# An encoder block on one core: the gated product gets a tile of its own, and the handling of w_down is tied to the rounds of the up projection

## Chip, cores, metric

One of the cores of a Trainium2 chip runs the whole program. The metric is the device time of one execution in microseconds (us). Engines are named as in the profile: PE (TensorE), DVE (VectorE), ACT (ScalarE), POOL (GpSimd), and SP, whose instruction queue issues every DMA of this kernel.

## What is computed

The block has three sub-layers: a mixer of a convolution group and an attention group, a cross-attention into 256 memory tokens, and a gated MLP. The change touches the last:

```python
def conv_gated_ffn(h, w_up, ffn_dw, ffn_dw_b, w_down):
    u = jnp.einsum("bsd,df->bsf", h, w_up)                 # h: 1024 tokens x 1024
    u = dwconv_centred(u, ffn_dw, ffn_dw_b)                # width 3 along the tokens
    gate, val = u[..., :D_FF], u[..., D_FF:]               # D_FF = 2816
    return jnp.einsum("bsf,fd->bsd", jax.nn.gelu(gate, approximate=True) * val, w_down)
```

All of it is float32. The kernel keeps that precision by splitting each operand into a high and a low part and doing three matmuls per product.

## The kernel before, in words

**Up projection.** The 2816 gate channels and the 2816 value channels are taken 128 at a time, in 22 *rounds* (`NF`). In a round the result for one channel block is a matrix `u` of 128 channels x 2 (gate, value) x 1024 tokens. The multiplication of [gate; value] weights by [first half; second half] of the model dimension and by two halves of the tokens is done with seven products instead of eight (Strassen's scheme in Winograd's form). Each product is 12 matmuls of 128 x 128 by 128 x 512, its result one PSUM bank (`psB`, 4 buffers). The right operands `b11, b21, b22, t1..t4` are made once, before the rounds; the left operands `a1, a2, a3, a22` are made in each round from the two loaded weight tiles `wg` and `wv`.

- `up_first(fi)` (L788): load `wg`, split it into `a1` (high part ACT, low part POOL), products p1 and p2. p1 is copied to `q`, p2 + q is the first half of the gate.
- `up_operands(fi)` (L803): load `wv`; POOL makes the sums `s12`, `s34`; `a_split` (L774) makes `a2` and `a3` (high part ACT, low part DVE) and `a22` (ACT, POOL).
- `up_finish(fi)` (L832): products p6, p5, p3, p7, p4. Their partial sums go through `q`, a tile of 128 x 1024 from the pool `tmpp` (4 buffers, also used by `s12` and `s34`), until both halves of `u` are there; then `conv3` (L822: one ACT and two DVE instructions into PSUM) on each half, gelu on ACT, and the product of the two, written over `u[:, 1]` (L859) and stored to DRAM as `act_d[fi]` (L860).

`u`, `a1`, `a2`, `a3` and `a22` share the pool `wp` of 7 buffers. `wg` and `wv` share `rawp` (3 buffers) with other raw tiles.

**Preparing the down projection.** It uses the same seven-product scheme and needs four differences of blocks of `w_down`. They are made during the up projection, in 22 pieces: `down_load(fi)` (L763) brings a piece of 512 KB into one half of `wd_b`, `down_sums(fi)` (L766) does four subtractions of 128 x 256 on DVE in place (L769), `down_store(fi)` (L771) writes it to `T_d` in DRAM. `wd_b` has two halves, so piece fi+2 is loaded when piece fi has been stored.

**Down projection.** Seven products m1, m2, m6, m7, m5, m4, m3, each a sum over 11 blocks `i` of 12 matmuls (L91 to L93, results `yd`). The left operands come from `acts`, eleven tiles that are loaded from `act_d` in two halves each (L895, L897) into buffers that the right operands of the up projection leave; the right ones (`st`, L913) come from `w_down` or `T_d`, two blocks a load. Each is split by one ACT (L930) and one DVE instruction (L920).

**What sets the order.** A list scheduler places the instructions on the five queues at compile time by a timeline of its own; each engine then runs its queue strictly in order, and waits are semaphores. Nothing in the code before ties `down_load`, `down_sums` and `down_store` to a round, so the scheduler sets them as soon as its timeline finds them possible.

Of the kernel before, what the change touches and what calls it, by code (L numbers as in the profile page):

```python
# [11 lines left out]
ALU = mybir.AluOpType  # L12
# [5 lines left out]
NF = 22  # L18
# [16 lines left out]
def encoder_block(ctx: ExitStack, tc: tile.TileContext, x, xT, mem, w_a, w_q, w_kv, w_mkv, w_mqT,  # L35
                  w_mo, w_out, w_up, w_down, cols, rows, g10, rope, out):
    nc = tc.nc
# [10 lines left out]
    def A(shape, name, dt=F32R):  # L48
        return ap.tile([128] + shape, dt, tag="a", name=name)

    def raw(name):
        return rawp.tile([128, 1024], F32, tag="raw", name=name)

    def tmp(name):
        return tmpp.tile([128, 1024], F32, tag="tmp", name=name)

    def psS(name):
        return psp.tile([128, 1024], F32, tag="S", name=name, bufs=2)

    def psB(name):  # L60
        return psp.tile([128, 512], F32, tag="B", name=name, bufs=4)
# [4 lines left out]
    def f(t):  # L66
        return t.bitcast(F32)
# [10 lines left out]
    def cc(i):  # L78
        return col[:, i:i + 1]
# [31 lines left out]
    def W(shape, name):  # L111
        return wp.tile([128] + shape, F32R, tag="w", name=name)
# [150 lines left out]
    for t in range(2):  # L263
        r = raw(f"mem{t}")
# [135 lines left out]
    for i in range(2):  # L400
        r = raw(f"wkv{i}r").rearrange("p (k n) -> p k n", k=4)
# [3 lines left out]
        for j in (2 * i, 2 * i + 1):  # L405
            r = raw(f"wq{j}r").rearrange("p (k n) -> p k n", k=2)
# [211 lines left out]
    def post_norm(y, gB, resid, name):  # L618
# [5 lines left out]
        nc.vector.tensor_tensor(out=t, in0=t, in1=resid, op=ALU.add)  # L624
        return t

    def load_raw(src, name):
        r = raw(name)
        nc.sync.dma_start(out=r, in_=src)
        return r  # L630

    def transpose_split(src, dh, dl, tt):
# [80 lines left out]
    def cross_gemm(t):  # L713
        y = psS("y2")
        tok_gemm(y, Ph[t // 4], Pl[t // 4], Uw, t % 4)
        return y, load_raw(x1_d[t], "x1r")
# [36 lines left out]
    act_d = drp.tile([NF, 128, 1024], F32, name="act_d")  # L753


    T_d = drp.tile([NF // 2, 128, 4, 512], F32, name="T_d")

    wd_b = A([2, 4, 256], "wd", F32)

    def down_slice(dr, fi):  # L760
        return dr[fi // 2, :, :, fi % 2 * 256:fi % 2 * 256 + 256]

    def down_load(fi):  # L763
        nc.sync.dma_start(out=wd_b[:, fi % 2], in_=down_slice(w_down, fi))

    def down_sums(fi):  # L766
        b11, b12, b22, b21 = [wd_b[:, fi % 2, b, :] for b in range(4)]
        for dst, in0, in1 in ((b11, b12, b11), (b12, b22, b12), (b22, b22, b11), (b21, b22, b21)):
            nc.vector.tensor_tensor(out=dst, in0=in0, in1=in1, op=ALU.subtract)  # L769

    def down_store(fi):  # L771
        nc.sync.dma_start(out=down_slice(T_d, fi), in_=wd_b[:, fi % 2])

    def a_split(dst, src, eng):  # L774
        nc.scalar.copy(out=dst[:, 0, :], in_=src)  # L775
        eng.tensor_tensor(out=dst[:, 1, :], in0=src, in1=f(dst[:, 0, :]), op=ALU.subtract)  # L776

    def product(ps, a, b):
        bh, bl = BO[b]
        for k in range(4):  # L780
            ks = slice(k * 128, k * 128 + 128)
            gemm3_multi([ps], (a[:, 0, ks], a[:, 1, ks]), [(bh[:, k, :], bl[:, k, :])], k == 0, k == 3)

    a22 = [None, None]
    H0, H1 = slice(0, 512), slice(512, 1024)
    ups, firsts, rgs = {}, {}, {}

    def up_first(fi):  # L788

        rg = rgs.pop(fi) if fi in rgs else load_raw(w_up[fi, 0], "wg")  # L790
        a1 = W([2, 2, 512], "a1")
        a_split(a1[:, 0], rg[:, H0], nc.gpsimd)
        a_split(a1[:, 1], rg[:, H1], nc.gpsimd)
        u = wp.tile([128, 2, 1024], F32, tag="w", name="u")
        q = tmp("q")
        p1, p2 = psB("p1"), psB("p2")
        product(p1, a1[:, 0], "b11")
        nc.scalar.copy(out=q[:, H0], in_=p1)
        product(p2, a1[:, 1], "b21")
        nc.vector.tensor_tensor(out=u[:, 0, H0], in0=p2, in1=q[:, H0], op=ALU.add)  # L800
        firsts[fi] = (rg, u, q)

    def up_operands(fi):  # L803

        rg, u, q = firsts.pop(fi)
        rv = load_raw(w_up[fi, 1], "wv")
        s12, s34 = tmp("s12"), tmp("s34")
        nc.gpsimd.tensor_tensor(out=s12[:, H0], in0=rv[:, H0], in1=rv[:, H1], op=ALU.add)
        nc.gpsimd.tensor_tensor(out=s12[:, H1], in0=s12[:, H0], in1=rg[:, H0], op=ALU.subtract)
        nc.gpsimd.tensor_tensor(out=s34[:, H0], in0=rg[:, H0], in1=rv[:, H0], op=ALU.subtract)  # L810
        nc.gpsimd.tensor_tensor(out=s34[:, H1], in0=rg[:, H1], in1=s12[:, H1], op=ALU.subtract)
        a2, a3 = W([2, 2, 512], "a2"), W([2, 2, 512], "a3")
        a_split(a2[:, 0], s12[:, H1], nc.vector)
        a_split(a2[:, 1], s12[:, H0], nc.vector)
        a_split(a3[:, 0], s34[:, H1], nc.vector)
        a_split(a3[:, 1], s34[:, H0], nc.vector)
        if fi % 2 == 0:
            a22[0] = W([2, 2, 512], "a22")
        a_split(a22[0][:, fi % 2], rv[:, H1], nc.gpsimd)
        ups[fi] = (a2, a3, a22[0][:, fi % 2], u, q)  # L820

    def conv3(fi, gv, u):  # L822
        ci = gv * NF + fi
        c = psS("c")
        nc.scalar.activation(out=c, in_=u[:, gv], func=AF.Identity, scale=cc(C_FDW + ci * 3 + 1), bias=cc(C_FDB + ci))  # L825
        nc.vector.scalar_tensor_tensor(out=c[:, 1:], in0=u[:, gv, :S - 1], scalar=cc(C_FDW + ci * 3), in1=c[:, 1:],  # L826
                                       op0=ALU.mult, op1=ALU.add)
        nc.vector.scalar_tensor_tensor(out=c[:, :S - 1], in0=u[:, gv, 1:], scalar=cc(C_FDW + ci * 3 + 2),
                                       in1=c[:, :S - 1], op0=ALU.mult, op1=ALU.add)
        return c  # L830

    def up_finish(fi):  # L832
        a2, a3, a22_, u, q = ups.pop(fi)

        def add(dst, ps, other, op=ALU.add, swap=False):
            nc.vector.tensor_tensor(out=dst, in0=other if swap else ps, in1=ps if swap else other, op=op)  # L836

        p6, p5 = psB("p6"), psB("p5")
        if fi == 0:
            product(p5, a2[:, 1], "t1")  # L840
        product(p6, a2[:, 0], "t2")
        add(q[:, H0], p6, q[:, H0])
        if fi:
            product(p5, a2[:, 1], "t1")
        add(q[:, H1], p5, q[:, H0])
        p3 = psB("p3")
        product(p3, a3[:, 0], "b22")
        add(u[:, 0, H1], p3, q[:, H1])
        p7 = psB("p7")
        product(p7, a3[:, 1], "t3")  # L850
        add(q[:, H0], p7, q[:, H0])
        add(u[:, 1, H1], p5, q[:, H0])
        cg = conv3(fi, 0, u)
        nc.scalar.activation(out=u[:, 0], in_=cg, func=AF.Gelu_apprx_tanh)
        p4 = psB("p4")
        product(p4, a22_, "t4")
        add(u[:, 1, H0], p4, q[:, H0], op=ALU.subtract, swap=True)
        cv = conv3(fi, 1, u)
        nc.vector.tensor_tensor(out=u[:, 1], in0=u[:, 0], in1=cv, op=ALU.mult)  # L859
        nc.sync.dma_start(out=act_d[fi], in_=u[:, 1])  # L860

    UP_PRE = 2
    for t in range(8):
        if t == 6:
            for fi in range(UP_PRE):
                rgs[fi] = load_raw(w_up[fi, 0], "wg")
        j = cross_norm(t, *cross_gemm(t))
        if t == 7:
            for fi in range(UP_PRE):
                up_first(fi)  # L870
        cross_operands(t, j)
    for fi in range(NF + 1):
        if fi < NF:
            if fi >= UP_PRE:
                up_first(fi)
            up_operands(fi)
        if fi == 0:
            down_load(0)
        else:
            down_store(fi - 1)  # L880
            up_finish(fi - 1)
        if fi < NF:
            down_sums(fi)
        if fi + 1 < NF:
            down_load(fi + 1)

# [205 lines left out]
```

## Time and profile before

| | us |
|---|---|
| median of 3 runs (1451.33 to 1456.73) | 1452.29 |
| profiled execution | 1453.6 |
| its span | 1451.5 |
| PE busy | 1383.5 (95%) |
| DVE busy | 1070.8 (74%) |
| ACT busy | 699.9 (48%) |
| POOL busy | 514.0 (35%) |

The span is the time from the first to the last instruction; around it lie 2.1 us. A stretch of the span is read with a table of windows (busy time and number of instructions of each engine, granted clock of PE, share of the DMA engines); an idle place with the timeline of an engine, which gives the idle time before an instruction and what ended it; and the way in which one delay leads to the next with the chain of work, followed back from the end.

### The profile page before, as it was taken

The numbers are of one execution on the slowest core, as the hardware profiler recorded it, in microseconds if no ns is written. First come the engines' busy times: TensorE is split into PE (matmuls) and PEld (weight loads), VectorE is DVE, ScalarE is ACT, GpSimd is POOL, SyncE is SP. The second block draws the span as 40 slices with busy tenths as digits, with TensorE's granted clock in tenths as the row PEclk, the third lists the DMA queues.
The fourth block names the chain that finished last, engine by engine and source line by source line (L and its number), as shares of the span: only waits on it lengthen the run. The fifth ranks groups of instructions, "written<-read, shape, count | busy, mean of one in ns | idle before, by whom it ended". The sixth has DMA issues, their size and how long they took to land.

```text
span 1451.5 us, 18836 instructions
## 1 busy us (share of the span) xinstructions
PE 1383.5 (95%) x7042; PEld 1167.5 (80%) x7042; DVE 1070.8 (74%) x1442; ACT 699.9 (48%) x1191; POOL 514.0 (35%) x506
## 2 busy tenths in 40 slices
PE   9999999799999999999996989789999999999996
PEld 7889988679898888888885767678888888888885
DVE  6699899799998334335458878877777778985576
ACT  7426543588888434334444424234444443544452
POOL 5548887600102324002136525345554441000003
PEclk9999999999999999999998999899999999999998
DMA  6417750000000434013223576742222228622325
GB/s 236 135 59 238 243 200 14 19 1 2 30 1 12 163 103 151 24 43 131 87 87 102 174 232 198 236 135 83 74 93 81 88 87 317 226 88 88 109 87 210
DMA packets 74060, 170.08 MB, mean 117 GB/s; under 512 B 9713, under 2 KB 32497, under 8 KB 73969
## 3 DMA queue, kind: packets, MB, share of 16 engines
q1 hardware_dynamic: 73968, 168.88, 35.1%
q8 instruction: 55, 0.90, 0.3%
q14 instruction: 37, 0.30, 0.1%
HBM read 124.82 MB, written 44.04 MB: 116 GB/s over the span
## 4 chain that ended last, share of the span: by engine, by line
PE 62%; DVE 7%; DMA 5%; ACT 2%; issue 2%; POOL 1%; POOLq 0%; DVEq 0%; ACTq 0%; SPq 0%
PE p L98 7%; PE p L99 6%; PE p L101 6%; PE yd L91 5%; PE yd L92 5%; PE yd L93 5%; PE y L99 4%; PE y L101 4%; PE y L98 4%; PE pPT L82 3%; DVE wd L769 3%; DMA wd<-in_w_down_dram 2%; DMA T_d<-wd 2%; PE sc L101 2%; PE sc L98 2%; PE sc L99 2%
## 5 line engine op out<-in xcount | busy, mean ns | idle before, releaser
L305 DVE SCALAR_TENSOR_TENSOR cacc<-conv,col,cacc 128x1009 f32<-128x1009 f32 (+14 forms) x120 | 145.8, 1276 | 4.7 <-ACT cacc L253 4.5
L86 POOL TENSOR_SCALAR rt<-ss 128x1 f32<-128x1 f32 (+1 forms) x43 | 15.0, 349 | 353.5 <-DVE ss L920 227.2
L92 PE MATMUL yd<-op 128*128 128x512 f32 x308 | 119.8, 389 | 0.0
L93 PE MATMUL yd<-op 128*128 128x512 f32 x308 | 119.7, 389 | 0.0
L775 ACT CAST a<-s 128x512 fp32r<-128x512 f32 x88 | 50.8, 621 | 105.6 <-PE p L101 65.1
L91 PE MATMUL yd<-op 128*128 128x512 f32 x308 | 96.9, 389 | 0.0
L930 ACT CAST op<-acts 128x512 fp32r<-128x512 f32 x77 | 48.0, 624 | 99.6 <-PE yd L93 87.8
L776 POOL TENSOR_TENSOR a<-wg,a 128x512 fp32r<-128x512 f32 x44 | 63.1, 1456 | 84.1 <-ACT a L775 84.0
L920 DVE TENSOR_TENSOR op<-acts,op 128x512 fp32r<-128x512 f32 x77 | 53.1, 690 | 46.5 <-ACT op L930 46.4
L826 DVE SCALAR_TENSOR_TENSOR c<-u,col,c 128x1023 f32<-128x1023 f32 x44 | 56.6, 1285 | 39.9 <-ACT c L825 39.9
L557 DVE TENSOR_TENSOR PL<-pPT,PH 128x512 fp32r<-128x512 f32 x128 | 83.2, 681 | 2.4 <-ACT PH L556 1.4
L539 DVE TENSOR_REDUCE nm<-sp 128x1 f32<-128x1024 f32 x64 | 78.0, 1218 | 7.3 <-PE sp L537 6.8
L825 ACT ACTIVATE c<-u,col 128x1024 f32<-128x1024 f32 x44 | 53.2, 1209 | 54.8 <-DVE u L836 53.4
L542 ACT ACTIVATE P<-sp,nm 128x1024 f32<-128x1024 f32 x64 | 72.2, 1128 | 15.4 <-PE pPT L82 6.5
L776 DVE TENSOR_TENSOR a<-s,a 128x512 fp32r<-128x512 f32 x88 | 67.0, 779 | 15.2 <-ACT a L775 15.0
L556 ACT CAST PH<-pPT 128x512 fp32r<-128x512 f32 x128 | 69.4, 593 | 13.9 <-PE pPT L82 13.4
L769 DVE TENSOR_TENSOR wd<-wd 128x256 f32<-128x256 f32 x88 | 57.0, 664 | 20.5 <-DMA wd<-in_w_down_dram 20.0
L82 PE MATMUL pPT<-ident,P 128*128 128x128 f32 x512 | 67.9, 273 | 0.7 <-DVE PL L557 0.7
L92 PEld LDWEIGHTS yd<-op 128*128 128x128 f32 x308 | 57.8, 188 | 12.4 <-DVE op L920 0.4
L91 PEld LDWEIGHTS yd<-op 128*128 128x128 f32 x308 | 57.8, 188 | 12.0
L93 PEld LDWEIGHTS yd<-op 128*128 128x128 f32 x308 | 57.8, 188 | 12.0
L776 POOL TENSOR_TENSOR a<-wv,a 128x512 fp32r<-128x512 f32 x22 | 32.9, 1513 | 97.5 <-ACT a L775 83.1
(344 smaller groups left out, 4395.1 us busy)
## 6 DMA issues: line engine op xcount, KB each, us to landing
wg<-in_w_up_dram SPq DMA_DIRECT2D x22, 512.0 KB, 4.4
wv<-in_w_up_dram SPq DMA_DIRECT2D x22, 512.0 KB, 4.2
wd<-in_w_down_dram SPq DMA_DIRECT2D x22, 512.0 KB, 4.2
T_d<-wd SPq DMA_DIRECT2D x22, 512.0 KB, 3.9
act_d<-u SPq DMA_DIRECT2D x22, 512.0 KB, 2.9
acts<-act_d SPq DMA_DIRECT2D x22, 512.0 KB, 6.8
st<-T_d SPq DMA_DIRECT2D x20, 512.0 KB, 3.7
wmkv_r<-in_w_mkv_dram SPq DMA_DIRECT2D x16, 512.0 KB, 4.1
```

The source lines that it names most:

```text
L82: nc.tensor.transpose(out=out_, in_=in_, identity=ident)
L91: nc.tensor.matmul(out=ps, lhsT=sh, rhs=mh, start=first, stop=False)
L92: nc.tensor.matmul(out=ps, lhsT=sh, rhs=ml, start=False, stop=False)
L93: nc.tensor.matmul(out=ps, lhsT=sl, rhs=mh, start=False, stop=last)
L98: nc.tensor.matmul(out=p, lhsT=sh, rhs=mh, start=first, stop=False)
L99: nc.tensor.matmul(out=p, lhsT=sh, rhs=ml, start=False, stop=False)
L101: ins = nc.tensor.matmul(out=p, lhsT=sl, rhs=mh, start=False, stop=last)
L305: nc.vector.scalar_tensor_tensor(out=acc[:, t0:t1_], in0=a[:, t0 + o:t1_ + o], scalar=cc(C_DW + c * 31 + j), in1=acc[:, t0:t1_], op0=ALU.m ...
L539: nc.vector.reduce_max(out=nm, in_=sp, axis=AX.X, negate=True)
L557: nc.vector.tensor_tensor(out=PL[dst], in0=p3, in1=f(PH[dst]), op=ALU.subtract)
L769: nc.vector.tensor_tensor(out=dst, in0=in0, in1=in1, op=ALU.subtract)
L776: eng.tensor_tensor(out=dst[:, 1, :], in0=src, in1=f(dst[:, 0, :]), op=ALU.subtract)
```

## The change

1. `q` is no longer a tile of `tmpp` but the value half of `u`, `u[:, 1, :]`. The gated product goes to a new tile `o` of `tmpp`, and `act_d[fi]` is stored from `o`.
2. `down_load` and `down_store` are queued on SP behind the last load of `wg` or `wv` that the program text issued (`issue_after` adds an edge of order on the engine's own queue, no semaphore).
3. `down_sums(fi + 1)` is called within `up_finish(fi)` and queued on DVE behind the addition of p7; piece 0 behind the last split of `up_operands(0)`. `down_store(fi - 2)` stands behind `up_first(fi)`, `down_load(fi)` behind `up_operands(fi)`; the last two stores follow the loop.

```diff
+    last_load = [None]
     def load_raw(src, name):
         r = raw(name)
-        nc.sync.dma_start(out=r, in_=src)
+        last_load[0] = nc.sync.dma_start(out=r, in_=src)
...
     def down_load(fi):
-        nc.sync.dma_start(out=wd_b[:, fi % 2], in_=down_slice(w_down, fi))
-    def down_sums(fi):
+        with tc.issue_after(last_load[0].ins):
+            nc.sync.dma_start(out=wd_b[:, fi % 2], in_=down_slice(w_down, fi))
+    def down_sums(fi, behind):
...
+        with tc.issue_after(behind.ins):
+            for dst, in0, in1 in ((b11, b12, b11), (b12, b22, b12), (b22, b22, b11), (b21, b22, b21)):
+                nc.vector.tensor_tensor(out=dst, in0=in0, in1=in1, op=ALU.subtract)
     def down_store(fi):
-        nc.sync.dma_start(out=down_slice(T_d, fi), in_=wd_b[:, fi % 2])
+        with tc.issue_after(last_load[0].ins):
+            nc.sync.dma_start(out=down_slice(T_d, fi), in_=wd_b[:, fi % 2])
...
         u = wp.tile([128, 2, 1024], F32, tag="w", name="u")
-        q = tmp("q")
+        q = u[:, 1, :]
...
-        add(q[:, H0], p7, q[:, H0])
+        seventh = add(q[:, H0], p7, q[:, H0])
         add(u[:, 1, H1], p5, q[:, H0])
+        if fi + 1 < NF:
+            down_sums(fi + 1, seventh)
...
-        nc.vector.tensor_tensor(out=u[:, 1], in0=u[:, 0], in1=cv, op=ALU.mult)
-        nc.sync.dma_start(out=act_d[fi], in_=u[:, 1])
+        o = tmp("o")
+        nc.vector.tensor_tensor(out=o, in0=u[:, 0], in1=cv, op=ALU.mult)
+        nc.sync.dma_start(out=act_d[fi], in_=o)
...
             if fi >= UP_PRE:
                 up_first(fi)
-            up_operands(fi)
-        if fi == 0:
-            down_load(0)
+                down_store(fi - 2)
+            lo = up_operands(fi)
+            down_load(fi)
+        if fi:
+            up_finish(fi - 1)
         else:
-            down_store(fi - 1)
-            up_finish(fi - 1)
-        if fi < NF:
-            down_sums(fi)
-        if fi + 1 < NF:
-            down_load(fi + 1)
+            down_sums(0, lo)
+    for fi in (NF - 2, NF - 1):
+        down_store(fi)
```

The number of instructions and of bytes moved stays the same; the order of the queues changes from the end of the cross-attention on. Three places show it (names carry the buffer's number; in the changed file the same lines stand some numbers lower in the text, L769 is L773, L836 is L842, L764 is L767, L772 is L777, L860 is L869, L913 is L921).

SP's queue in the early rounds, before (`wd` and `T_d`: pieces of w_down; `wg`, `wv`: up weights; `act_d`: the round's result):

```order
L772 DMA T_d_6643<-wd_6644 512x1x256 x2
L764 DMA wd_6644<-in_w_down_dram 128x4x256 x2
L772 DMA T_d_6643<-wd_6644 512x1x256
L629 DMA wv_8064<-in_w_up_dram 128x1024
L764 DMA wd_6644<-in_w_down_dram 128x4x256
L860 DMA act_d_6642<-u_7597 128x1024
L772 DMA T_d_6643<-wd_6644 512x1x256
L764 DMA wd_6644<-in_w_down_dram 128x4x256
L629 DMA wg_8172<-in_w_up_dram 128x1024
L772 DMA T_d_6643<-wd_6644 512x1x256
```

and in the changed kernel:

```order
L777 DMA T_d_6643<-wd_6644 512x1x256
L869 DMA act_d_6642<-o_8457 128x1024
L631 DMA wv_8643<-in_w_up_dram 128x1024
L767 DMA wd_6644<-in_w_down_dram 128x4x256
L631 DMA wg_8751<-in_w_up_dram 128x1024
L777 DMA T_d_6643<-wd_6644 512x1x256
L869 DMA act_d_6642<-o_8603 128x1024
```

Before, two or three pieces of w_down stand between two results; now each round has one store, one result, one `wv`, one piece, one `wg`, and the same five in every round from the fourth to the twentieth.

DVE's queue where round 0 begins to be finished, before:

```order
L776 TENSOR_TENSOR a2_7490<-s12_7484,a2_7490 128x512
L769 TENSOR_TENSOR wd_6644<-wd_6644 128x256 x6
L836 TENSOR_TENSOR q_7365<-p6_7503,q_7365 128x512
L769 TENSOR_TENSOR wd_6644<-wd_6644 128x256
L836 TENSOR_TENSOR q_7365<-p5_7504,q_7365 128x512
L776 TENSOR_TENSOR a2_7490<-s12_7484,a2_7490 128x512
L769 TENSOR_TENSOR wd_6644<-wd_6644 128x256
L776 TENSOR_TENSOR a3_7491<-s34_7485,a3_7491 128x512 x2
L836 TENSOR_TENSOR u_7364<-p3_7531,q_7365 128x512
```

and in the changed kernel:

```order
L781 TENSOR_TENSOR a2_7487<-s12_7481,a2_7487 128x512 x2
L781 TENSOR_TENSOR a3_7488<-s34_7482,a3_7488 128x512 x2
L842 TENSOR_TENSOR u_7364<-p6_7500,u_7364 128x512
L773 TENSOR_TENSOR wd_6644<-wd_6644 128x256
L842 TENSOR_TENSOR u_7364<-p5_7501,u_7364 128x512
L773 TENSOR_TENSOR wd_6644<-wd_6644 128x256
L842 TENSOR_TENSOR u_7364<-p3_7528,u_7364 128x512
L842 TENSOR_TENSOR u_7364<-p7_7542,u_7364 128x512
L773 TENSOR_TENSOR wd_6644<-wd_6644 128x256 x2
```

Six subtractions stood ahead of the first partial sum; now none does, and one stands between p6's and p5's.

SP's queue at the passage to the down projection, before (`acts`: left operands, L895 first halves, L897 second halves; `st_10623`, `st_10659`, `st_10695`, `st_10731`, `st_10767`, `st_10803` are the right operands of m1 in the order of use, two blocks each):

```order
L897 DMA acts_10588<-act_d_6642 128x1024
L897 DMA acts_10590<-act_d_6642 128x1024
L913 DMA st_10767<-in_w_down_dram 128x2x512
L913 DMA st_10659<-in_w_down_dram 128x2x512
L913 DMA st_10731<-in_w_down_dram 128x2x512
L895 DMA acts_10592<-act_d_6642 128x1024
```

and in the changed kernel (`gF` is a row of gains; `o_10494` is the result of round 20, of which the second half of `acts_10600` is a reload):

```order
L921 DMA st_10832<-in_w_down_dram 128x2x512
L903 DMA acts_10602<-act_d_6642 128x1024
L907 DMA gF_10615<-in_rows_dram 128x1024
L869 DMA act_d_6642<-o_10494 128x1024
L905 DMA acts_10600<-act_d_6642 128x1024
L921 DMA st_10659<-in_w_down_dram 128x2x512
L921 DMA st_10731<-in_w_down_dram 128x2x512
```

The second, fourth and sixth of m1's right operands moved from the middle of the loads of `acts` to behind the last of them but one, and behind the store of round 20.

## Rows read from the trace of the kernel before

**Rows 1.** Windows of the up projection: us, PE, PEld, DVE, ACT, POOL, clock, DMA share, GB/s.

```profile
798.90:970.00 171.10, 147.43 (x607) 116.76 (x608) 143.75 (x204) 58.53 (x81) 70.15 (x53) 0.95 0.62 200
970.00:1218.00 248.00, 248.00 (x1092) 205.32 (x1091) 180.57 (x213) 103.44 (x143) 117.06 (x88) 1.00 0.31 102
798.90:1230.50 431.60, 407.93 (x1752) 332.43 (x1753) 336.74 (x434) 167.21 (x229) 187.22 (x140) 0.98 0.45 148
```

**Rows 2.** PE's timeline: start, us, line, matmul, [idle before and what ended it].

```profile
803.67 0.47 PE L98 MATMUL p<-b11h,a 128*128 128x512 f32 x1 [1.76 <-DVE u L836]
849.31 0.80 PE L98 MATMUL p<-b11h,a 128*128 128x512 f32 x1 [5.49 <-ACT a L775]
```

**Rows 3.** The chain of work through one stall: start, us, what.

```profile
836.97 7.19 DMA wd<-in_w_down_dram
...
846.81 0.61 DVE u L836
...
848.72 0.55 ACT a L775
...
851.47 0.43 PE p L98
...
857.60 0.23 PE p L98
```

**Rows 4.** Waits from 798 to 970: waited for, us in total, times, longest.

```profile
ACT a L775 <- DMA act_d<-u: 29.3, 5, 10.8
ACT a L775 <- PE p L101: 27.5, 10, 4.3
...
DVE wd L769 <- DMA wd<-in_w_down_dram: 20.0, 11, 5.0
```

**Rows 5.** Windows with only the instructions on wd: us, DVE busy, clock, DMA share.

```profile
798.90:970.00 171.10, 51.45 (x82) 0.95 0.62 200
```

**Rows 6.** DVE's timeline at round 0 and at two groups of subtractions.

```profile
791.75 1.11 DVE L776 TENSOR_TENSOR a<-s,a 128x512 fp32r<-128x512 f32 x1 [3.09 <-ACT a L775]
792.78 5.37 DVE L769 TENSOR_TENSOR wd<-wd 128x256 f32<-128x256 f32 x6
798.08 0.68 DVE L836 TENSOR_TENSOR q<-p,q 128x512 f32<-128x512 f32 x1
...
814.11 0.75 DVE L769 TENSOR_TENSOR wd<-wd 128x256 f32<-128x256 f32 x2
...
828.98 5.05 DVE L769 TENSOR_TENSOR wd<-wd 128x256 f32<-128x256 f32 x5
```

**Rows 7.** POOL's timeline at the same places.

```profile
795.51 1.35 POOL L811 TENSOR_TENSOR s<-wg,s 128x512 f32<-128x512 f32 x1
...
820.80 2.66 POOL L776 TENSOR_TENSOR a<-wv,a 128x512 fp32r<-128x512 f32 x2 [9.95 <-ACT a L775]
...
830.51 1.47 POOL L809 TENSOR_TENSOR s<-s,wg 128x512 f32<-128x512 f32 x1
```

**Rows 8.** DMA issues: what, times, KB each, median us to landing.

```profile
wd<-in_w_down_dram SPq DMA_DIRECT2D x22, 512.0 KB, 4.2
T_d<-wd SPq DMA_DIRECT2D x22, 512.0 KB, 3.9
act_d<-u SPq DMA_DIRECT2D x22, 512.0 KB, 2.9
```

**Rows 9.** The tile st: ns min/median/max, first and last start; then us to landing.

```profile
L920 DVE TENSOR_TENSOR op<-st,op x77: 677/686/698, 1217.4 to 1427.5; 128x512 fp32r<-128x512 f32 x77
...
DMA to landing us min/median/max: 2.9/3.8/12.6
```

**Rows 10.** SP's timeline at the passage to the down projection.

```profile
1207.36 4.18 SPq L913 DMA_DIRECT2D st<-in_w_down_dram  x3
...
1229.57 0.33 SPq L899 DMA_DIRECT2D gF<-in_rows_dram  x1
1230.87 0.33 SPq L860 DMA_DIRECT2D act_d<-u  x1
```

More of the change, by code (lines that the diff above doesn't have):

```diff
@@ L763, in down_load @@
     def down_load(fi):
-        nc.sync.dma_start(out=wd_b[:, fi % 2], in_=down_slice(w_down, fi))
-    def down_sums(fi):
+        with tc.issue_after(last_load[0].ins):
+            nc.sync.dma_start(out=wd_b[:, fi % 2], in_=down_slice(w_down, fi))
+    def down_sums(fi, behind):
         b11, b12, b22, b21 = [wd_b[:, fi % 2, b, :] for b in range(4)]
-        for dst, in0, in1 in ((b11, b12, b11), (b12, b22, b12), (b22, b22, b11), (b21, b22, b21)):
-            nc.vector.tensor_tensor(out=dst, in0=in0, in1=in1, op=ALU.subtract)
+        with tc.issue_after(behind.ins):
+            for dst, in0, in1 in ((b11, b12, b11), (b12, b22, b12), (b22, b22, b11), (b21, b22, b21)):
+                nc.vector.tensor_tensor(out=dst, in0=in0, in1=in1, op=ALU.subtract)
     def down_store(fi):
-        nc.sync.dma_start(out=down_slice(T_d, fi), in_=wd_b[:, fi % 2])
+        with tc.issue_after(last_load[0].ins):
+            nc.sync.dma_start(out=down_slice(T_d, fi), in_=wd_b[:, fi % 2])
     def a_split(dst, src, eng):
         nc.scalar.copy(out=dst[:, 0, :], in_=src)
-        eng.tensor_tensor(out=dst[:, 1, :], in0=src, in1=f(dst[:, 0, :]), op=ALU.subtract)
+        return eng.tensor_tensor(out=dst[:, 1, :], in0=src, in1=f(dst[:, 0, :]), op=ALU.subtract)
     def product(ps, a, b):
@@ L815, in up_operands @@
         a_split(a3[:, 0], s34[:, H1], nc.vector)
-        a_split(a3[:, 1], s34[:, H0], nc.vector)
+        lo = a_split(a3[:, 1], s34[:, H0], nc.vector)
         if fi % 2 == 0:
@@ L820, in up_operands @@
         ups[fi] = (a2, a3, a22[0][:, fi % 2], u, q)
+        return lo
     def conv3(fi, gv, u):
@@ L835, in add @@
         def add(dst, ps, other, op=ALU.add, swap=False):
-            nc.vector.tensor_tensor(out=dst, in0=other if swap else ps, in1=ps if swap else other, op=op)
+            return nc.vector.tensor_tensor(out=dst, in0=other if swap else ps, in1=ps if swap else other, op=op)
         p6, p5 = psB("p6"), psB("p5")
```

## Prediction

> **What bounds the kernel now.** I read the table of windows first. In the up projection PE is the engine that counts, and there are two stretches. From 970 to 1218 PE is busy in all 248.00 us, at full granted clock (1.00, the 2.4 GHz level): 1092 matmuls, so 0.2271 us each, and nothing done elsewhere can shorten it. From 798.9 to 970 it is busy for 147.43 of 171.10 us [rows 1]. Over both, 1752 matmuls (146 products of 12) take 431.6 us where 1752 x 0.2271 = 397.9 would do. So 33.7 us are lost, all before 970: 431.6 - 407.93 = 23.7 us idle, and 10.0 us in which the matmuls run, but slowly.
>
> PE's timeline shows what the losses are: stalls at round ends, such as 1.76 us ended by DVE's partial sum and 5.49 us ended by ACT's split of `a1` [rows 2]. The chain of work through the one of 5.49 us begins far away. A load of a piece of w_down takes 7.19 us; the subtraction that waits for it stands in DVE's queue ahead of a3's low parts and p3's addition (846.81); behind that addition ACT starts the convolution, and only then splits `a1`, for which PE waits [rows 3]. After the stall the matmuls follow each other every 0.43 us, the 1.2 GHz level, and are back at 0.23 by 857.60 [rows 3]: that is the 10.0 us. So the chain of load, subtractions and store of w_down, which is independent of the rounds, runs as fast as it can and sits in the queues ahead of the rounds' own work. The waits say the same: DVE stood 20.0 us for its loads, ACT 29.3 us for stores of `act_d` (SP's queue holds those up, and the buffer of `u` is not free until they land) [rows 4]. And 82 subtractions cost DVE 51.45 us of 171 there [rows 5]; DVE is busy in 84% of that stretch, in 73% of the next [rows 1]. By 970 the chain is done, and so are the stalls.
>
> **The change, part by part.**
>
> *Opening.* The first product of round 2 starts at 803.67 and waits for DVE [rows 2], which first has to add p6 of round 0, at 798.08. Ahead of that stand six subtractions, 5.37 us, and an idle time of 3.09 us for ACT's split of round 1 [rows 6]. In the new queue none of the six stands there. POOL now makes three of round 0's four sums before an operand subtraction, and round 1's `wv` can leave earlier, so I take the 3.09 away too: p6's addition 8.5 us earlier, at 789.6. But then a subtraction waits for its load. Piece 0 now stands in SP's queue behind `wv` of round 2, whose buffer POOL frees when it ends at 796.9 [rows 7], 8.5 earlier 788.4. With two issues of about 0.33 [rows 10] and a landing of 4.2 [rows 8] it is there at 793.2. Two subtractions of 0.37, the additions of p5 and p3 at 0.6 to 0.68 [rows 6]: PE starts round 2 at 795.3, 8.4 us earlier. Between 0 (the wait for the piece eats it all) and 11.5 (no wait).
>
> *Rounds.* From 803.67 to 1230.5, 145 products lie on PE's path: 1740 x 0.2271 = 395.2 of 426.8 us, 31.6 lost. A round is 84 matmuls, 19.08 us. DVE needs 180.57 / 248 x 19.08 = 13.9 us of it [rows 1], and with four subtractions of 51.45 / 82 = 0.63 [rows 5] 16.4: 2.7 to spare. A piece's load is queued a round and a half ahead of its subtractions, some 28 us, against 3.9 for the store before it and 4.2 for itself [rows 8], so DVE should not stand for it any more. `u` is free when DVE has written `o`; the 29.3 us of ACT's waits [rows 4] go, without the store. `o`, `s12` and `s34` share four buffers as `q`, `s12`, `s34` did, but `o` is held for one instruction and a store of 2.9 us [rows 8], `q` was for two rounds: no cost. The work of the moved DMAs is the same 44 x 512 KB, now at 31% DMA share plus its own, hidden. So the stalls go; I leave 2 us of them (0 to 8, the upper end below), a gain of 29.6.
>
> *Passage to the down projection.* Here I see a new wait. m1's second pair of right operands was issued by 1212 [rows 10], before half of the left ones. It now stands behind `gF`, the store of round 20 and a reload that must wait until this store has landed. Let E be the end of the last up product (1230.5 before). `gF` went out at E - 0.9 and that store at E + 0.4 [rows 10]; 2.9 to land [rows 8], the reload at E + 3.3, the pair at E + 3.7; 3.8 to land, a split of 0.6 on ACT and 0.69 on DVE [rows 3, 9]: ready at E + 8.8. The first pair keeps PE for 24 x 0.2271 = 5.5 us. So PE stands 3.3 us; after the stall of 5.49 the matmuls ran at half speed for at most 857.6 - 849.3 = 8.3 us, which costs up to 4 [rows 2, 3]; with somewhat less than half of that I take 5. Bounds 0 and 12, the latter by the longest landing of such an operand, 12.6 [rows 9].
>
> *Everything else* costs nothing: the additions have the same operands in number and size, one from PSUM, and the number of instructions is unchanged.
>
> *Sum:* 8.4 + 29.6 - 5 = 33.0. Against the profiled execution: 1453.6 - 33.0 = 1420.6; that one lies 1.3 us above the median, so **1419**.
>
> **Rivals.**
>
> *The subtractions collide with POOL in every round (slower than forecast, 0.15).* Two of them took 0.75 us at 814.11 while POOL stood idle (for 9.95 us until 820.80), five took 5.05 us at 828.98 while POOL was adding [rows 6, 7]: 0.37 against 1.01. POOL's instructions last 1.35 to 1.47 us [rows 7], and if each subtraction has to sit one out, four cost 5.6 us, DVE needs 13.9 + 5.6 = 19.5 of 19.08 us and becomes the bound: 0.4 x 19 rounds = 8 us, time 1427. Against it: POOL is busy in 117.06 of 248 us [rows 1], 47%, and the average of 0.63 already has such meetings in it. The Trainium skill (SBUF — State Buffer, section "SBUF: two separate sides") has a rule for this: a VectorE instruction with two SBUF inputs and a GpSimd instruction that reads SBUF share one pair of ports under an exclusive lock, and the later one is blocked for the whole instruction of the other. By that rule, spreading the subtractions over rounds in which POOL works speaks against the change; the trace agrees with it at the two places named.
>
> *Slower than before (0.06).* The pieces come late in every round: `act_d` waits in SP's queue for `o`, and `wv`, the piece and `wg` stand behind it. Then DVE stands at the first subtraction, with the second addition of p5, p4's, the convolution and the next `o` behind it, and the delay feeds itself. The longest such wait was 5.0 us [rows 4]; less the 2.7 to spare, 2.3 us in each of 20 rounds is 46 us: 1465. It decides from a wait of 2.7 + 33.0 / 20 = 4.4 us in each round. Against it speak the 28 us of lead.
>
> *It does not do what it says (0.06).* The stalls could come from `wp`'s seven buffers alone: ACT also waited 27.5 us for products that free `a1` or `a2` [rows 4], and nothing adds a buffer. Then they return wherever they were, and the time is 1452. Against it: after 970 the buffers are the same and PE never stands [rows 1].
>
> **How the numbers follow.** The forecast has 0.73, the port rival 0.15, the other two 0.06 each. Best end: 11.5 + 31.6 - 0 = 43, 1409. Worst end within the forecast: 0 + 23.6 - 12 = 12, 1441, which needs all three at once; I stop at 1436, which takes in the port rival with a late start of m1. About 0.5%, 7 us, is what a measurement can tell from no change: faster 0.88 (forecast and port rival), same 0.06, slower 0.06.
>
> **What would show it.** PE without stalls from round 2 to the end of the rounds, E near 1192; four subtractions in every round between p7's addition and the convolution of the value half, and no wait of DVE for `wd` after round 1; no wait of ACT for `act_d` in the rounds; full granted clock from about 800. At m1, one stall of 3 to 5 us at the third block, ended by DVE's split of the second pair. Wrong would be: stalls at round ends that DVE or ACT ends, subtractions of 1 us and more in most rounds, or a first product of round 2 later than 800.

## The result, and the profile after

The changed kernel takes **1435.5 us** (median of 4 runs, 1434.9 to 1436.6); the kernel before took 1454.5 in the runs beside it. The ratio is 0.987, with a 95% interval of 0.985 to 0.990: faster by 1.3%. The forecast was 1419 in a range of 1409 to 1436, so the direction holds, and the size is at the range's slow end: 19 us came of the 33 forecast. The profiled executions are 18.6 us apart (1453.6 and 1435.0), and it is these 18.6 that can be followed.

Three marks cut an execution into stretches: the first product of the up projection (the first matmul on `b11h`), the first product of round 2, and the first matmul of the down projection (`yd`, E in the prediction). A fourth, the first product of `t4` in round 0, lies just ahead of the second and is used where the opening alone is compared. The rows of the three tiles in the lines of the profile have the first and the last start in us behind the durations. Before the change:

```profile
L98 PE MATMUL p<-b11h,a x88: 389/389/795, 758.0 to 1200.4; 128*128 128x512 f32 x88
L98 PE MATMUL p<-t4h,a x88: 389/389/500, 798.9 to 1229.8; 128*128 128x512 f32 x88
L91 PE MATMUL yd<-op x308: 388/389/393, 1230.5 to 1439.6; 128*128 128x512 f32 x154
```

and after it:

```profile
L98 PE MATMUL p<-b11h,a x88: 387/389/482, 756.8 to 1165.8; 128*128 128x512 f32 x88
L98 PE MATMUL p<-t4h,a x88: 389/389/468, 798.5 to 1195.4; 128*128 128x512 f32 x88
L91 PE MATMUL yd<-op x308: 387/389/796, 1196.1 to 1421.4; 128*128 128x512 f32 x154
```

Round 2's first product after the change, from PE's timeline:

```profile
801.29 0.43 PE L98 MATMUL p<-b11h,a 128*128 128x512 f32 x1
```

| us | before | after | gain | forecast |
|---|---|---|---|---|
| first up product to round 2's first | 758.0 to 803.67 [rows 2]: 45.7 | 756.8 to 801.29: 44.5 | 1.2 | 8.4 |
| round 2's first to E | to 1230.5: 426.8 | to 1196.1: 394.8 | 32.0 | 29.6 |
| E to the last `yd` start | 209.1 | 225.3 | -16.2 | -5 |
| what lies ahead and behind | 772.0 | 770.4 | 1.6 | 0 |

The last line is no effect of the change that I can name: the first up product started anywhere from 756.6 to 760.3 in the executions of the kernels below, so starts are compared from that mark on.

The windows of after show where PE works and where it doesn't (the columns of [rows 1]):

```profile
801.20:970.00 168.80, 168.80 (x746) 139.54 (x745) 153.51 (x183) 73.33 (x100) 87.25 (x61) 1.00 0.44 146
970.00:1190.00 220.00, 220.00 (x972) 182.07 (x971) 198.39 (x237) 90.70 (x126) 110.23 (x76) 1.00 0.46 155
1190.00:1200.00 10.00, 9.24 (x40) 7.00 (x38) 10.00 (x15) 3.49 (x4) 0.00 (x0) 1.00 1.02 382
1200.00:1210.00 10.00, 5.58 (x12) 3.53 (x12) 9.93 (x15) 4.46 (x6) 0.00 (x0) 0.63 0.82 329
1210.00:1220.00 10.00, 4.43 (x12) 3.39 (x12) 9.27 (x14) 3.46 (x7) 0.00 (x0) 0.52 0.91 281
1220.00:1230.00 10.00, 10.00 (x46) 8.25 (x45) 5.31 (x9) 3.42 (x6) 0.00 (x0) 1.00 0.59 197
```

From round 2 to 1190 PE is busy all the time at full clock, where it stood 23.7 us and ran slowly for a while before [rows 1, 2]. Then come thirty bad microseconds: from 1190 to 1220 PE is busy 19.25 of 30.00 and does 64 matmuls, for which 64 x 0.2271 = 14.5 would do. So 10.75 us are idle and 4.7 are lost to the clock (0.52 to 0.63 granted). PE's timeline has the stalls, those of the opening first:

```profile
774.45 0.79 PE L98 MATMUL p<-t1h,a 128*128 128x512 f32 x1 [3.07 <-ACT t1h L709]
777.15 0.79 PE L99 MATMUL p<-t1l,a 128*128 128x512 f32 x1 [1.91 <-DVE t1l L710]
787.47 0.79 PE L99 MATMUL p<-t3l,a 128*128 128x512 f32 x1 [3.74 <-DVE t3l L710]
...
1202.42 0.67 PE L91 MATMUL yd<-op 128*128 128x512 f32 x1 [3.07 <-DVE u L842]
1207.22 0.80 PE L91 MATMUL yd<-op 128*128 128x512 f32 x1 [2.00 <-DVE u L842]
1215.72 2.07 PE L91 MATMUL yd<-op 128*128 128x512 f32 x4 [5.57 <-ACT op L938]
```

The two at the start of m1 wait for PSUM banks, which the last partial sums of the rounds free. The third waits for the split of the second pair of right operands. SP's timeline shows when that pair left (the first of the four at 1209.73), ACT's when it was split:

```profile
1200.59 0.32 SPq L869 DMA_DIRECT2D act_d<-o  x1
1209.36 0.32 SPq L905 DMA_DIRECT2D acts<-act_d  x1
1209.73 2.78 SPq L921 DMA_DIRECT2D st<-in_w_down_dram  x4
```

```profile
1214.53 0.62 ACT L938 CAST op<-acts 128x512 fp32r<-128x512 f32 x1 [3.72 <-DVE o L868]
1215.05 1.14 ACT L938 CAST op<-st 128x512 fp32r<-128x512 f32 x2
```

Between the store of round 20 and the reload that waits for its landing lie 8.8 us; four loads of right operands stand behind that reload, the pair among them. The load was not the only limit: it had landed by 1214.2 (4.5 us behind 1209.73), but ACT's split of it, at 1215.05, stood behind a split that waited until 1214.53 for DVE's last product. So DVE's backlog held the third block as long as the load did, to within 0.9 us.

### The profile page after: what moved, and what is told of

It reads as the page before. It is cut to its first block, busy times and chain, and to the rows that moved or that the text cites. A ratio compares the mean times of both kernels' runs of the same rounds, so it can differ in the third digit from the quotient of the medians.

```text
span 1433.2 us, 18843 instructions
## 1 busy us (share of the span) xinstructions
PE 1380.4 (96%) x7042; PEld 1167.0 (81%) x7042; DVE 1100.7 (77%) x1442; ACT 700.3 (49%) x1191; POOL 529.0 (37%) x506
## 4 chain that ended last, share of the span: by engine, by line
PE 67%; DVE 6%; ACT 2%; issue 2%; DMA 1%; POOL 1%; SPq 0%; POOLq 0%; DVEq 0%; ACTq 0%
PE p L101 8%; PE p L99 8%; PE p L98 8%; PE yd L91 5%; PE yd L92 5%; PE yd L93 5%; PE y L99 4%; PE y L101 4%; PE y L98 4%; PE pPT L82 3%; PE sc L101 2%; PE sc L98 2%; PE sc L99 2%; PE sp L536 2%; PE po L567 2%
## 5 line engine op out<-in xcount | busy, mean ns | idle before, releaser
L92 PE MATMUL yd<-op 128*128 128x512 f32 x308 | 121.4, 395 | 0.0
L93 PE MATMUL yd<-op 128*128 128x512 f32 x308 | 121.1, 394 | 0.0
L91 PE MATMUL yd<-op 128*128 128x512 f32 x308 | 103.0, 397 | 10.7 <-ACT op L938 5.6
L781 POOL TENSOR_TENSOR a<-wg,a 128x512 fp32r<-128x512 f32 x44 | 68.3, 1574 | 62.1 <-ACT a L780 62.1
L781 DVE TENSOR_TENSOR a<-s,a 128x512 fp32r<-128x512 f32 x88 | 87.8, 1037 | 0.0
L842 DVE TENSOR_TENSOR u<-p,u 128x512 f32<-128x512 f32 x110 | 75.0, 683 | 6.0 <-PE p L101 5.0
L832 DVE SCALAR_TENSOR_TENSOR c<-u,col,c 128x1023 f32<-128x1023 f32 x44 | 56.5, 1284 | 29.3 <-ACT c L831 29.2
```

Of the source, the lines that this page charges most:

```text
L91: nc.tensor.matmul(out=ps, lhsT=sh, rhs=mh, start=first, stop=False)
L92: nc.tensor.matmul(out=ps, lhsT=sh, rhs=ml, start=False, stop=False)
L93: nc.tensor.matmul(out=ps, lhsT=sl, rhs=mh, start=False, stop=last)
L781: return eng.tensor_tensor(out=dst[:, 1, :], in0=src, in1=f(dst[:, 0, :]), op=ALU.subtract)
L842: return nc.vector.tensor_tensor(out=dst, in0=other if swap else ps, in1=ps if swap else other, op=op)
```

## Experiments

Edits are against the changed kernel. The stretches are those of the table above, each from its kernel's own profiled execution; the time is the median of the runs.

| kernel | time, us | ratio to before (95%) | first up product to E | E to last `yd` start |
|---|---|---|---|---|
| before | 1454.5 | | 472.5 | 209.1 |
| the change | 1435.5 | 0.987 (0.985 to 0.990) | 439.3 | 225.3 |
| tie alone | 1445.3 | 0.993 (0.991 to 0.994) | 461.8 | 210.2 |
| tile alone | 1462.5 | 1.005 (1.003 to 1.007) | 465.5 | 225.3 |
| m2's sums held back | 1432.6 | 0.985 (0.983 to 0.986) | 441.5 | 220.9 |
| two pairs of operands early | 1431.7 | 0.984 (0.982 to 0.985) | 439.1 | 220.0 |
| reloads behind too | 1431.1 | 0.983 (0.981 to 0.985) | 438.9 | 220.1 |
| opening's sums on DVE | 1435.2 | 0.986 (0.984 to 0.988) | 434.1 | 227.9 |
| the last two together | 1426.1 | 0.980 (0.979 to 0.982) | 435.4 | 220.1 |
| last two products in `u` | 1422.4 | 0.979 (0.978 to 0.981) | 439.1 | 210.9 |
| the same, with the opening's sums on DVE | 1417.2 | 0.975 (0.974 to 0.977) | 436.2 | 211.0 |

### Each half of the change by itself

The tie alone:

```diff
-        q = u[:, 1, :]
+        q = tmp("q")
...
-        o = tmp("o")
-        nc.vector.tensor_tensor(out=o, in0=u[:, 0], in1=cv, op=ALU.mult)
-        nc.sync.dma_start(out=act_d[fi], in_=o)
+        nc.vector.tensor_tensor(out=u[:, 1], in0=u[:, 0], in1=cv, op=ALU.mult)
+        nc.sync.dma_start(out=act_d[fi], in_=u[:, 1])
```

> Only the w_down chain is tied to the rounds; the partial sums stay in a tile of their own and the gated product in u, which is stored from there (as before the change). If the untied chain alone made the stalls (my theory): PE has no stall of over 1 us from the third round to the end of the last up product E, E falls from 1230.5 to between 1195 and 1200, and the time is 1425 to 1438, the lower end if the right operands of m1, which leave earlier here, spare the third stall of the down projection. If the buffer of u, held by the store of act_d, made them (rival): ACT again waits some 25 us or more for act_d in the rounds, stalls of 2 to 5 us return, and the time is over 1442.

The tile alone is the reverse of it: these three places as in the change, all of w_down's loads, sums and stores as before.

> Only the gated product gets a tile of its own and the partial sums move into u; the loads, subtractions and stores of w_down run as fast as they can, as before the change. If the chain made the stalls (my theory): they stay, DVE still stands some 30 us for pieces of w_down before 970, PE loses over 20 us there, and the time is 1445 to 1456. If u's buffer made them (rival): no wait of ACT for act_d, no stalls, time under 1437.

Neither half does it. The tie alone shortens the stretch from the first up product to E by 10.7 us, the tile alone by 7.0, both together by 33.2. With the tie alone the stalls of round ends are smaller (0.7 to 1.8 us, with a second one of 0.73 behind each), but from 984 on they come in every second round up to 1188, where before the change there was none after 970. ACT's wait shows why, and so does SP's timeline at the stores:

```profile
ACT a L780 <- DMA act_d<-u: 88.7, 19, 5.9
```

```profile
995.66 0.34 SPq L868 DMA_DIRECT2D act_d<-u  x1
1016.00 0.33 SPq L868 DMA_DIRECT2D act_d<-u  x1
1036.34 0.34 SPq L868 DMA_DIRECT2D act_d<-u  x1
```

From the store at 834.18 to that at 1178.78, 17 rounds later, they are 20.3 us apart at the mean, where a round of 84 matmuls takes 19.08; 1.2 more in each of some 18 rounds is the difference of 22.5 us to the whole change. The chain of work over 985 to 1010 is a loop: product, store (6.04 us), ACT's split into the buffer that it held, convolution, sums, the next product. Its largest shares:

```profile
by line: DMA act_d<-u 24.2%; DVE wd L773 23.6%; DVE c L832 10.0%; DVE c L834 9.8%; DVE u L842 9.5%; issue 5.4%; DVE q L842 4.7%; DVE u L867 4.6%; ACT a L780 4.6%; ACT c L831 4.5%; DVE u L805 2.7%; DVE a L781 2.4%; ACTq L780 0.2%
```

So the rival of that run's expectation, that `u`'s buffer makes the stalls, is right for the tied kernel. In the tile alone the other half is right: ACT no longer waits for `act_d`, but the chain of w_down still stalls the rounds (PE busy 162.1 of the 180 us from 800 to 980; 156.3 before the change), though DVE stands only 13.9 us for its pieces, where I had expected some 30. The tile alone ends above the 1456 that I gave as the upper bound, because of its passage, 225.3 us as in the whole change. PE's timeline there:

```profile
1227.95 0.50 PE L91 MATMUL yd<-op 128*128 128x512 f32 x1 [0.61 <-DVE u L836]
1233.34 0.80 PE L91 MATMUL yd<-op 128*128 128x512 f32 x1 [3.74 <-DVE u L836]
1243.49 2.07 PE L91 MATMUL yd<-op 128*128 128x512 f32 x4 [7.22 <-ACT op L931]
```

No sum of w_down stands in DVE's queue at that place, and the loss is the same. So the passage's loss belongs to the tile, not to the sums that the tie puts late.

### Which part of w_down's work the tied loop can't bear

Two runs of the tie alone, with a part of that work left out. Without the subtractions:

```diff
-        if fi + 1 < NF:
+        if fi + 1 < 2:
             down_sums(fi + 1, seventh)
```

> The kernel with the tie alone, without the four subtractions on w_down's pieces from piece 2 on (part of the computation is left out; loads and stores remain). From the first up product to the first down product it took 461.8 us with them, 439.3 in the changed kernel. If DVE's extra 2.5 us a round make the product, and so the store that holds u's buffer, late (theory): the stretch falls to 438 to 446. If the DMA traffic of w_down makes that store slow (6.0 us) and that alone decides (rival): 455 or more.

Without the transfers:

```diff
-                down_store(fi - 2)
+                if fi < 4:
+                    down_store(fi - 2)
             lo = up_operands(fi)
-            down_load(fi)
+            if fi < 2:
+                down_load(fi)
...
-    for fi in (NF - 2, NF - 1):
+    for fi in range(2, NF):
         down_store(fi)
```

> The kernel with the tie alone, without the loads and stores of w_down's pieces from piece 2 on in the rounds (the stores follow in a row behind the last round, of no meaningful data, so the time itself says nothing); the subtractions remain. If DVE's extra work decides (theory): the stretch from the first up product to the first down product stays at 455 or more up to the last two rounds. If the DMA traffic decides (rival): ACT's wait for the store of act_d falls from 88.7 us to under 40, and the stretch falls below 446.

The stretch came to 439.4 us without the subtractions and to 439.7 without the transfers: both at the whole change's 439.3, and PE without a stall from 860 to 1160 in both. So without the subtractions the theory came true, and without the transfers the rival did: it is not DVE's extra work alone. Either part alone fits into the loop, only both together exceed the round. ACT's wait for the store is 39.8 us in 10 waits without the subtractions, and 4.8 in 3 without the transfers:

```profile
ACT a L780 <- DMA act_d<-u: 39.8, 10, 4.3
```

```profile
ACT a L780 <- DMA act_d<-u: 4.8, 3, 4.0
```

The whole change takes the store out of the loop instead, and then has room for both.

### The passage to the down projection

First DVE was relieved: the three combinations that m2 prepares are held behind m1's last split.

```diff
         if name == "m2":
-            comb(V_, a21, a21, a22, ALU.add)
-            comb(V_, a11, a21, a11)
-            comb(V_, a12, a12, a11)
+            with tc.issue_after(last_split[0].ins):
+                comb(V_, a21, a21, a22, ALU.add)
+                comb(V_, a11, a21, a11)
+                comb(V_, a12, a12, a11)
```

> The changed kernel, with the three combinations of acts that m2 prepares for m6, m7 and m5 held behind m1's last split on DVE, so that DVE comes to the last partial sums of round 21 earlier. E stays near 1196. If DVE's backlog makes the stalls at the start of the down projection (theory): the first two, 3.1 and 2.0 us ended by the last partial sum, shrink to under 2 together, ACT's copies follow, the third one (5.6 us) falls below 3, and the time is 1424 to 1430. If the late load of m1's second pair of right operands makes the third stall and the slow clock after it (rival, the mechanism of my prediction): the third stall stays at 5 us or more and the time is 1432 to 1437.

The first two stalls went, and one of 10.16 us stands in the place of the third:

```profile
1216.15 2.08 PE L91 MATMUL yd<-op 128*128 128x512 f32 x4 [10.16 <-ACT op L940]
```

The third block starts 15.8 us behind E, where it was 19.6 in the change; but E came late (1200.4, and not near 1196 as expected), so that only 2.2 of the passage's 4.4 us are left up to the last `yd` start. The time, 1432.6, is that of the rival: with DVE out of the way the load of the right operands sets the stall, as the chain of work shows.

```profile
1204.87 10.59 DMA st<-in_w_down_dram
```

It was not a reload that held this load back, though: here the pair left at 1204.87, 6.5 us ahead of the reload (1211.33), and took 10.6 us to land. Next, m1's first two pairs were loaded ahead of the last two stores of `act_d` and of `gF`:

```diff
+        if fi == NF - 1:
+            for n, pool in enumerate((raw, tmp)):
+                st = pool("st").rearrange("p (i n) -> p i n", i=2)
+                first_st.append((st, nc.sync.dma_start(
+                    out=st, in_=w_down[2 * n:2 * n + 2, :, 0, :].rearrange("i p n -> p i n"))))
```

(with the last two stores and `gF` queued behind the second of them, and m1 taking its first four blocks from `first_st`).

> The changed kernel, with m1's first two pairs of right operands loaded ahead of the last two stores of act_d and of gF. E stays near 1196. If that late load makes the third stall (the mechanism of my prediction): the third stall goes, the two before it stay at about 5 us together, and the time is 1425 to 1430. If DVE's backlog makes it (rival): a stall of 4 us or more in the third block stays, ended by ACT or DVE, and the time is 1433 to 1437.

```profile
1203.05 0.50 PE L91 MATMUL yd<-op 128*128 128x512 f32 x1 [1.09 <-DVE u L842]
1221.48 2.07 PE L91 MATMUL yd<-op 128*128 128x512 f32 x4 [5.98 <-ACT op L950]
```

The stall in the third block is gone, but one of 5.98 us came up four blocks further on (1203.05 is in the second block, 1221.48 begins the seventh, with m1's fourth pair). The two stalls before it, which were expected to stay at about 5 us together, shrank to the 1.09 as well. The time lies between the two theories. Behind the reload (1212.29) the loads of right operands went on at 1213.22, when DVE had made a split that frees a buffer; so the run does not say which of the two waits held the fourth pair. To see whether it was the reload, the reloads of the last two rounds were put behind all of m1's right operands:

```diff
+            if name == "m1" and i + n == NH:
+                with tc.issue_after(d.ins):
+                    second_half(NH - 2)
+                    second_half(NH - 1)
+                    nc.sync.dma_start(out=gF[:, 0, :], in_=...)
```

> As the run before with m1's first two pairs of right operands loaded early, and besides this the reloads of the last two rounds' act_d (which m1 does not read) and gF stand behind all of m1's right operands in SP's queue. If the loads of right operands that stand behind the first such reload, which waits for its store to land, make the stall of 6 us in the fifth block (theory): that stall goes or falls under 2 us, the passage (first down product to the last one's start, 209.1 us before the change, 225.3 after it, 220.0 in the run with two pairs early) falls to 210 to 214, and the time is 1422 to 1427. If DVE's backlog of partial sums sets the passage (rival): another stall of 4 us or more, ended by DVE, takes its place, the passage stays at 218 or more, and the time is 1430 to 1434.

That missed: 1431.1 us and a passage of 220.1, the numbers of the rival, and a stall of 3.79 us at the same block. (The expectation's "fifth block" is the seventh.) The fourth pair left no earlier:

```profile
1202.41 0.32 SPq L872 DMA_DIRECT2D act_d<-o  x1
1214.40 1.41 SPq L934 DMA_DIRECT2D st<-in_w_down_dram  x3
```

Ahead of it in SP's queue now stood a load for m2, which needs the buffer of an m1 operand and waited for DVE's split of it until 1214.4. The order of the queue had changed, and the pair still stood behind a wait. The order follows the buffers: `o` of the last rounds sits in the pool from which every second pair of right operands takes its own. So the gated product of the last two rounds went back to `u`:

```diff
-        o = tmp("o")
+        o = u[:, 1] if fi >= NF - 2 else tmp("o")
```

> The changed kernel, but the gated product of the last two rounds goes into u again and is stored from there, so that the two buffers of o come free for right operands; in SP's queue all six pairs for m1 then stand ahead of the store of round 20 and its reload. If the right operands' place in SP's queue makes the loss at the start of the down projection (theory): from the first down product to the last one's start 209 to 213 us instead of 225.3 (209.1 before the change, 210.2 with the tie alone, 225.3 with the tile alone), and the time is 1420 to 1425. If it is DVE's backlog of partial sums or the full DMA queues (rival): 218 or more, 1430 or more.

```profile
1175.45 0.42 SPq L869 DMA_DIRECT2D act_d<-o  x1
1176.49 11.51 SPq L921 DMA_DIRECT2D st<-in_w_down_dram  x5
...
1204.08 0.32 SPq L869 DMA_DIRECT2D act_d<-u  x1
```

All of m1's pairs left before E, the passage fell to 210.9 us, and the one stall left in it is of 1.27 us. The time is 1422.4, as the theory had it. DVE was no emptier than in the change (38.86 us busy from 1200 to 1240; 29.25 there, with PE's stalls) and the DMA queues as full (share 0.82 from 1160 to 1200; 0.80 there); the five loads of 512 KB of right operands that left between 1174.8 and 1189 even took 12.3 us to land at the median. So neither sets the passage by its amount of work. The edit changed DVE's order too: the last two additions of the rounds came 2.5 and 7.3 us behind E instead of 5.6 and 10.4, and the two stalls that they ended are gone. How much each of the two orders gave back is not shown.

### The opening

In the opening 8.4 us were forecast and 1.2 came. DVE's timeline of the changed kernel, with POOL's beside it:

```profile
775.34 1.75 DVE L710 TENSOR_TENSOR t1l<-r_b,t1h 128x512 fp32r<-128x512 f32 x1
...
781.70 5.72 DVE L710 TENSOR_TENSOR t3l<-r_b,t3h 128x512 fp32r<-128x512 f32 x4
...
790.72 0.68 DVE L710 TENSOR_TENSOR t2l<-r_b,t2h 128x512 fp32r<-128x512 f32 x1
...
797.63 0.69 DVE L842 TENSOR_TENSOR u<-p,u 128x512 f32<-128x512 f32 x1 [1.22 <-PE p L101]
```

```profile
781.95 1.58 POOL L813 TENSOR_TENSOR s<-wv 128x512 f32<-128x512 f32 x1 [0.83 <-issue]
783.49 1.71 POOL L815 TENSOR_TENSOR s<-wg,wv 128x512 f32<-128x512 f32 x1
```

The addition of p6 (797.63) did lose the six subtractions ahead of it [rows 6], but it comes 40.8 us behind the first up product, as against 40.1 before: it is no earlier. DVE stood ready 1.22 us before it; p6 itself was late, as PE had stood 3.74 us for the split of `t3` (787.47 above) and had a granted clock of 0.50 (the 1.2 GHz level) from 787 to 793. Operand splits take 1.75 us there where others of the same size take 0.6 to 0.7 (790.72), and POOL works beside the long ones. Before the change `t3`'s four splits had taken 4.52 us, beside POOL's sums of round 0; POOL's sums of round 1, which began at 789.8 then, now begin at 781.95 and run beside them. To test that, DVE made these sums:

```diff
-        nc.gpsimd.tensor_tensor(out=s12[:, H0], ...)
+        eng = nc.vector if fi < UP_PRE else nc.gpsimd
+        eng.tensor_tensor(out=s12[:, H0], ...)
```

(and so for the other three).

> The changed kernel, with the four operand sums of rounds 0 and 1 made by DVE instead of POOL. That adds 8 instructions of about 0.6 us to DVE between 770 and 797. If DVE's instructions took 1.75 us there because POOL read SBUF beside them (theory): they take 0.6 to 0.7 again, 13 of them save about 14 us against the 5 added, and p6 of round 0 is added at 790 to 795 instead of 797.6; the time is 1429 to 1433, if POOL's other sums take no part. If DVE's queue is simply too full there (rival): the addition comes at 800 to 803 and the time is 1437 to 1442.

```profile
785.34 2.49 DVE L710 TENSOR_TENSOR t3l<-r_b,t3h 128x512 fp32r<-128x512 f32 x4
...
794.97 1.40 DVE L843 TENSOR_TENSOR u<-p,u 128x512 f32<-128x512 f32 x2
```

With eight instructions more on DVE, the four splits of `t3` take 2.49 us instead of 5.72, p6 is added 35.8 us behind the first up product instead of 40.8, and round 2 begins 39.5 us behind it (798.65) instead of 44.5. The stretch to E is 5.2 us shorter. The collision is shown, a gain in time is not: 1435.2 us misses the expected 1429 to 1433 and can't be told from the change's 1435.5. This profiled execution gave 2.6 us back in the passage (227.9) and began its up projection 2.4 us later. Together with the reloads behind:

> The two edits before this together: they touch places 400 us apart, so if both theories hold the gains add up: 1416 to 1424. If only the passage moves: 1422 to 1427.

1426.1 us: 5.0 less than without the opening's edit, but above the range, since the passage still had its 220.1. And with the passage cured:

> The edit before this together with the opening's sums on DVE, which shortened the stretch from the first up product to the first product of t4 from 41.7 to 36.6 us. If both hold and nothing takes the gain back: 1415 to 1420. If the passage takes the opening's 5 us back, as in the run with that edit alone: 1420 to 1425.

**1417.2 us**, 5.2 less than without the opening's edit. The profiled executions show a part of that gain: the stretch to E is 2.9 us shorter here (436.2 and 439.1) and 3.5 in the pair before (435.4 and 438.9). The one here took 1420.65, the longest of its four. This version is faster than before by 2.5% (interval 2.3 to 2.6%) and than the change as it stands by about 18 us.

## Why the prediction was right or wrong

**Rounds: right.** 32.0 us came of the 31.6 that were lost; I had left 2.0 for stalls that did not come back. The mechanism is shown from both sides: the tile without the tie keeps the stalls, the tie without the tile spreads them. What I did not see is how much the two need each other. I credited the 29.3 us of ACT's waits [rows 4] as a part of the gain; in truth the store's hold on `u` is what would have taken over had only the chain been tied.

**Port collisions: right in kind, smaller in the rounds than the rival had it.** DVE's groups from 801 to 1190, before the change and after (count, then busy us and mean ns):

```profile
L776 DVE TENSOR_TENSOR a<-s,a 128x512 fp32r<-128x512 f32 x77 | 58.2, 773 | 10.3 <-ACT a L775 10.1
L769 DVE TENSOR_TENSOR wd<-wd 128x256 f32<-128x256 f32 x81 | 50.7, 639 | 20.5 <-DMA wd<-in_w_down_dram 20.0
L836 DVE TENSOR_TENSOR q<-p,q 128x512 f32<-128x512 f32 x56 | 38.3, 684 | 3.8 <-PE p L101 3.5
```

```profile
L781 DVE TENSOR_TENSOR a<-s,a 128x512 fp32r<-128x512 f32 x80 | 80.5, 1046 | 0.0
L842 DVE TENSOR_TENSOR u<-p,u 128x512 f32<-128x512 f32 x104 | 70.9, 683 | 4.7 <-PE p L101 3.8
L773 DVE TENSOR_TENSOR wd<-wd 128x256 f32<-128x256 f32 x85 | 63.1, 744 | 0.6
```

The subtractions went from 639 to 744 ns, the splits, which I had left at their old price, from 773 to 1046. Additions with one operand from PSUM stay where they were, at 683 (684 before). DVE is busy in 153.51 of 168.80 us, so 17.4 of a round's 19.08, where I had worked out 16.4 and the rival 19.5. It did not become the bound in the rounds. The Trainium skill (SBUF — State Buffer, section "SBUF: two separate sides") has DVE instructions with two SBUF inputs and POOL instructions that read SBUF lock each other out. That DVE's instructions with both operands in SBUF became longer, and its additions with one operand in PSUM did not, agrees with it.

**Opening: the step that failed is "p6's addition 8.5 us earlier".** I took the subtractions away and moved POOL's sums forward, as the queue shows, but left DVE's splits there at their old durations, and took DVE's queue for the limit, where PE's own late p6 was. The addition came 0.7 us later, counted from the first up product, and round 2's first product at 801.29: past 800, which the prediction names as a sign of being wrong. I had priced the collision for the subtractions in the rounds, as a rival, and not for the opening, where the change itself moves POOL's work beside work that PE waits for. With the sums off POOL the opening takes 39.5 us, 6.2 less than before, of the 8.4 forecast.

**Passage: the late pair came as forecast, but mis-sized and not alone; 16.2 us against 5, beyond my upper bound of 12.** Three things in the working of that term were wrong. The store of round 20 did not leave at E + 0.4 but at E + 4.5 (1200.59), because DVE came later to `o`; it landed not in 2.9 us [rows 8] but in 8.8, and held the reload behind it as long (the two stores of `act_d` between 1190 and 1225 landed in 7.9 us at the median, with the DMA share at 0.82 to 1.02); and the pair was not the only thing late: the last partial sums held PSUM banks for 3.07 and 2.00 us more, and DVE's last product held up ACT's split about as long as the load did. So a median landing time of the whole program was taken into a stretch in which 14 of the 22 loads of `acts` go out (1185 to 1222), and one stall was counted where there are three, with the half clock from the first to the last of them.

The trace of the kernel before had the landing time at the very place. There the store of round 20 left at 1230.87 [rows 10] and landed 10.2 us later, and its reload followed at 1241.14:

```profile
1241.14 0.34 SPq L897 DMA_DIRECT2D acts<-act_d  x1
```

With 10.2 in place of 2.9 the working's stall of 3.3 us would have been 10.6.

**Sum.** By the same steps: 1.2 + 32.0 - 16.2 + 1.6 = 18.6 us. Of the 14.4 us by which the forecast was too good, 11.2 lie in the passage and 7.2 in the opening, less 2.4 better rounds and 1.6 outside. That the time still lies in the range, half a microsecond from its end, is in part luck: the passage alone went 4.2 us past its bound, and the better rounds and the 1.6 us that nothing explains made up for it.

## What to carry to other kernels

When an independent chain of loads and sums overruns a loop, tying it to the loop's rounds gives its full gain only if the loop has room for it: look for the buffer whose release goes through a store, and take that out of the loop with the same change. A tile moved into another pool takes a buffer from that pool's next tenants, so follow the pool beyond the loop to the stage behind, where an in-order queue may now hold a load behind a wait. Take the landing time of a transfer from the stretch where it will run, not from the whole program. And measure stage by stage from a common mark, since a total that moves by 19 us may be a gain of 33 less a loss of 16.

## What the runs showed of the hardware that was not expected

A DVE instruction of 128x512 with both operands in SBUF took 0.68 us alone and 1.75 beside POOL, so that eight instructions more on DVE, in place of POOL's, made the stretch to E 2.9 to 5.2 us shorter. And the stores of `act_d`, which land in 3.1 us at the median of all 22, took 7.9 in the stretch where the DMA share stood at up to 1.02 with 382 GB/s. In the version with the right operands ahead their loads took longer still to land (12.3 us at the median), and the passage was 14.4 us shorter: there the order of the queues counted for more than the duration of one transfer.
